# First expert's rows by one-hot products instead of a gather over DRAM, and the last row tile's affine part on TensorE and ScalarE

## The chip, the cores and the metric

One core of one Trainium2 chip runs the whole program. The metric is the time of one execution in device microseconds (us). The engines are named as in the profile: PE (TensorE, with PEld for its weight loads), DVE (VectorE), ACT (ScalarE), POOL (GpSimd) and SP (SyncE, which issues most transfers).

## The reference

One layer of an encoder on 512 tokens of 1024 channels. A token mixer (three linear-attention branches, merged by gates) ends in an output projection; its sum with the scaled input is normalised. A router then sends each token to two of 16 experts, each with two input matrices 1024 x 256 and one output matrix 256 x 1024; the weighted sum is added to the scaled tokens and normalised again. The part that matters here:

```
    mix = hybrid_mixer(h, ...)                     # ends in y @ w_out
    h = layer_norm(ALPHA * h + mix, ln1_g, ln1_b)  # the rows that are routed
    ffn = grouped_moe(h, ...)
    h = layer_norm(ALPHA * h + ffn, ln2_g, ln2_b)

def grouped_moe(x, ...):
    scores = sigmoid(t @ w_router)
    sel = (scores + router_bias).reshape(-1, 4, 4)          # 4 groups of 4 experts
    group_score = top_k(sel, 2)[0].sum(-1)                  # the best group,
    ...                                                     # the 2 best experts in it
    combine = one-hot of the 2 experts, times their scores over the sum
    h = silu(t @ w_gate[e]) * (t @ w_up[e])
    y = sum over e of (h * combine[e]) @ w_down[e]
```

## The kernel before

The 512 tokens are four row tiles of 128. The output projection is done in two column halves of 512. In the second half, `for n in range(NT)`, row tile n has four units (`wo_mm`, six matmuls each, float32 split in a high and a low part); between the units the steps of earlier row tiles are called. All instructions of this loop on TensorE are "pinned": each stays in its engine's queue behind the instruction that was written before it. Instructions that are not pinned are ordered by the framework's scheduler, by when their inputs are ready in its model.

`ln1(n)` holds the steps of one row tile: `half` adds the projection's result out of PSUM and takes statistics; `logits` transposes the tile and multiplies by the router; `scores` finds mean and inverse root and the sigmoid scores; `rows` applies gain and bias and stores the tile to `h1d` in DRAM. For the last tile 256 columns of the affine part run on DVE and 768 on ACT and POOL (multiply by the gain at L1263, add the bias at L1279).

`choose(n0, n1)` finds the experts of two row tiles on DVE: the mask `Mb`, and start values of `pos`; its inner `weigh` works out the weights. `ranks` multiplies the masks by a triangular matrix on PE and adds the result to `pos`, the place of a token among those of its expert. `slots` turns places into token numbers: for each expert a one-hot matrix (place equals slot, L1425) and small products of three columns (L1427, and L1436 for the weights). `gather` then fetches an expert's rows from `h1d` by an indirect transfer that POOL issues (L1449), and `ex_in` transposes them on PE (L1475).

`ex_up` multiplies by the input matrices in four units, each after a `split` of its raw weights into a high part (ACT, L316) and a low part (DVE, L317) in a ring of three pages. `ex_down` does the output matrix and scatters the result to `y2d` (L1507). The loop runs `ex_up(e)`, then `ex_down` of the expert before, then fetches the next expert. Raw weights come through a ring of 31 pages, so that about five experts are in stock when the loop begins. Between the last projection matmul and the first expert 66 matmuls on constants (L1536), which have no result that is used, are put on PE.

A float32 product appears in the trace as two matmuls each; a transpose as one.

Of the kernel before, what the change touches and what calls it, by code (L numbers as in the profile page):

```python
# [19 lines left out]
P = 128  # L20
# [18 lines left out]
def kernel(  # L39
# [1172 lines left out]
    raws = Ring(4)  # L1212
    for t in (whs, wls):
        t.i += 1
    def ln1(n):
# [12 lines left out]
        def half(c, psw):  # L1228
            cs = slice(c * T, (c + 1) * T)
            W.tensor_add(t[:, cs], t[:, cs], psw)  # L1230
            W.bn_stats(st[:, c], t[:, cs])

# [56 lines left out]
        return half, logits, scores, rows  # L1289
# [59 lines left out]
    def ranks():  # L1349

        ps = pst(pm)
        for n in range(NT):
# [4 lines left out]
        V.tensor_add(pos, pos, ps[:, :NT * E].rearrange("p (n e) -> p n e", e=E))  # L1357
# [18 lines left out]
    for n in range(NT):  # L1376
# [17 lines left out]
    half, logits, scores, rows = lns[3]  # L1394
    scores()
    rows()
    weigh = choose(2, 4, Pinned(V))
    ranks()
    drop(*x4)
    drop(*ah, *yT[0], *yT[1], g1r, b1r)  # L1400
# [7 lines left out]
    noh = [0]  # L1408
    raws = Ring(len(freed[F32]))
# [6 lines left out]
    def slots(es, pv, cv, gi, si, wi, mid=None, V=V):  # L1416

        m = len(es)
        ps, psw = pst(pm), pst(pm)
        oh = []  # L1420
        for j, e in enumerate(es):
# [4 lines left out]
            for n in range(NT):  # L1426
                TE.matmul(ps[:, 3 * j:3 * j + 3], o[:, n], cv(n, e)[:, 0:3], start=n == 0, stop=n == NT - 1)  # L1427
# [260 lines left out]
```

## Time and profile before

| | |
|---|---|
| median of 3 runs | 892.54 us (892.23 to 893.98) |
| the profiled execution, its own time | 893.27 us |
| its span | 891.6 us |
| mean granted clock of TensorE | 0.976 |
| PE busy | 831.9 us, 93% |
| DVE busy | 603.5 us, 68% |
| ACT busy | 442.3 us, 50% |
| POOL busy | 173.5 us, 19% |
| transfers | 126.05 MB, mean 141 GB/s |

The span reaches from the first to the last instruction that the profile records; the execution's own time is 1.7 us longer. Busy shares are means over stages with different limits. Mixer and branches take the first 620 us; the output projection ends at 670.55 us of the span, the experts run from about 691 to 860 us, and the last sum and normalisation take the rest.

### The profile page before, as it was taken

Reading aid. Unit: us, or ns where it says so; the run is one execution under the profiler, and the core shown is the slowest. Engines: PE = TensorE matmul, PEld = TensorE weight load, DVE = VectorE, ACT = ScalarE, POOL = GpSimd, SP = SyncE. Lnnn points to the kernel's source line nnn. Section 1 sums busy time; section 2 is a strip of 40 time slices with the busy share of each in tenths; the row PEclk is TensorE's granted clock in tenths of the full one; section 3 lists DMA queues with packets and bytes.
Section 4 is the critical chain, followed back from the end, with each engine's and each line's share of the span. In section 5 each row is a group of like instructions: output and inputs, shape, how many; then the busy total and the mean of one; then the engine's idle time right before and its main releaser. Section 6 shows DMA issues by size and latency. Waiting matters only on the chain.

```text
span 891.6 us, 15174 instructions
## 1 busy us (share of the span) xinstructions
PE 831.9 (93%) x5861; PEld 691.5 (78%) x5861; DVE 603.5 (68%) x1099; ACT 442.3 (50%) x823; POOL 173.5 (19%) x196
## 2 busy tenths in 40 slices
PE   8989999999989999999999999999998899999940
PEld 5867778978887999988888888888774777877730
DVE  7775566777675546686934346454469899989948
ACT  6533466654466443465323223233221688888833
POOL 2550001440361330201000000000023232222132
PEclk9989999999999999999999999999999999999985
DMA  6512322022013221244634334436635899997043
GB/s 196 136 54 74 86 69 60 25 75 70 25 72 119 72 71 49 72 129 133 187 111 127 95 98 142 119 119 214 234 119 172 269 364 353 362 365 289 27 168 134
DMA packets 100139, 126.05 MB, mean 141 GB/s; under 512 B 13072, under 2 KB 86880, under 8 KB 100064
## 3 DMA queue, kind: packets, MB, share of 16 engines
q1 hardware_dynamic: 89344, 109.17, 38.2%
q0 software_dynamic: 4608, 8.40, 2.6%
q10 hardware_dynamic: 6112, 7.48, 2.6%
q8 instruction: 47, 0.77, 0.4%
q14 instruction: 28, 0.23, 0.1%
HBM read 118.73 MB, written 14.68 MB: 150 GB/s over the span
## 4 chain that ended last, share of the span: by engine, by line
PE 70%; DVE 10%; issue 7%; DMA 5%; ACT 4%; POOL 3%; SPq 0%; DVEq 0%; ACTq 0%; POOLq 0%
PE ps L332 19%; PE ps L333 18%; PE ps L334 18%; PE ps L144 4%; DVE rr L317 2%; PE ps L906 1%; DMA ff<-in_w_gate_dram 1%; DVE ff L144 1%; PE ps L934 1%; PE ps L651 1%; PE ps L936 1%; PE ps L893 1%; ACT rr L316 1%; DMA ff<-in_w_down_dram 1%; POOL ff L713 1%
## 5 line engine op out<-in xcount | busy, mean ns | idle before, releaser
L317 DVE TENSOR_TENSOR rr<-ff,rr 128x1024 fp32r<-128x1024 f32 x148 | 183.4, 1246 | 117.3 <-ACT rr L316 114.5
L316 ACT CAST rr<-ff 128x1024 fp32r<-128x1024 f32 x150 | 157.0, 1054 | 178.6 <-PE ps L333 122.5
L332 PE MATMUL ps<-rh,rr 128*128 128x512 f32 x384 | 153.7, 400 | 0.0
L333 PE MATMUL ps<-rh,rr 128*128 128x512 f32 x384 | 150.5, 392 | 0.0
L334 PE MATMUL ps<-rh,rr 128*128 128x512 f32 x384 | 150.4, 392 | 0.0
L332 PE MATMUL ps<-rr,rh 128*128 128x256 f32 (+1 forms) x320 | 93.8, 293 | 0.6 <-DVE rh L144 0.6
L334 PE MATMUL ps<-rr,rh 128*128 128x256 f32 (+1 forms) x320 | 92.3, 289 | 1.5 <-issue 1.5
L333 PE MATMUL ps<-rr,rh 128*128 128x256 f32 (+1 forms) x320 | 91.9, 287 | 0.0
L332 PEld LDWEIGHTS ps<-rh,rr 128*128 128x128 f32 x384 | 72.4, 189 | 15.5 <-issue 0.8
L334 PEld LDWEIGHTS ps<-rh,rr 128*128 128x128 f32 x384 | 72.4, 189 | 15.5
L333 PEld LDWEIGHTS ps<-rh,rr 128*128 128x128 f32 x384 | 72.6, 189 | 14.1
L332 PEld LDWEIGHTS ps<-rr,rh 128*128 128x128 f32 x320 | 61.6, 192 | 3.2 <-issue 1.9
L334 PEld LDWEIGHTS ps<-rr,rh 128*128 128x128 f32 x320 | 61.3, 192 | 1.4 <-issue 0.8
L333 PEld LDWEIGHTS ps<-rr,rh 128*128 128x128 f32 x320 | 61.6, 193 | 0.3
L333 PE MATMUL ps<-rr,ro 128*128 128x512 f32 x128 | 52.2, 408 | 1.1 <-POOL rr L317 0.6
L332 PE MATMUL ps<-rr,ro 128*128 128x512 f32 x128 | 51.7, 404 | 0.3 <-issue 0.2
L334 PE MATMUL ps<-rr,ro 128*128 128x512 f32 x128 | 51.2, 400 | 0.7 <-DVE ro L1478 0.7
L1285 POOL TENSOR_TENSOR ff<-ff,ff 128x1024 f32<-128x1024 f32 x1 | 2.4, 2379 | 225.4 <-PE ps L144 225.4
L334 PE MATMUL ps<-ro,rr 128*128 128x512 f32 x96 | 37.4, 389 | 0.0
L332 PE MATMUL ps<-ro,rr 128*128 128x512 f32 x96 | 37.3, 389 | 0.0
L333 PE MATMUL ps<-ro,rr 128*128 128x512 f32 x96 | 37.3, 389 | 0.0
L1507 POOL DMA_INDIRECT y2d<-fl,sidx x16 | 20.8, 1300 | 71.5 <-ACT fl L1506 58.4
(550 smaller groups left out, 1681.8 us busy)
## 6 DMA issues: line engine op xcount, KB each, us to landing
ff<-in_w_in_dram SPq DMA_DIRECT2D x66, 512.0 KB
ff<-in_w_down_dram SPq DMA_DIRECT2D x25, 512.0 KB
ff<-in_w_gate_dram SPq DMA_DIRECT2D x41, 256.0 KB
ff<-in_w_up_dram SPq DMA_DIRECT2D x41, 256.0 KB
fh<-in_w_gate_dram SPq DMA_DIRECT2D x18, 256.0 KB
fh<-in_w_up_dram SPq DMA_DIRECT2D x18, 256.0 KB
ff<-in_w_out_dram SPq DMA_DIRECT2D x8, 512.0 KB
fh<-in_w_down_dram SPq DMA_DIRECT2D x6, 512.0 KB
```

The lines of the kernel that those rows point to most:

```text
L144: return lambda *a, **k: pin(f(*a, **k))
L316: S.copy(a, src)
L317: i = V.tensor_sub(b, src, a.bitcast(F32))
L332: TE.matmul(ps, w(0, k), h(0, k), start=start and k == k0, stop=False)
L333: TE.matmul(ps, w(0, k), h(1, k), start=False, stop=False)
L334: last = TE.matmul(ps, w(1, k), h(0, k), start=False, stop=stop and k == k1 - 1)
L651: tiny = lambda ps, lhs, rhs: [TE.matmul(half(ps)[u, i], lhs[u, i], rhs[u, i], start=True, stop=True) for i in range(NL) for u in B32]
L713: G.tensor_mul(ktok, ktok, bcol(ksc, NL))
L893: TE.matmul(p4[:, :, n], kd[:, g * NT + n], qd[:, g * NT + n], start=True, stop=True)
L906: TE.matmul(ps[:, c], kd[:, c], qd[:, c], start=True, stop=True)
L934: TE.matmul(po, atv(h)[:, n], vs[h][:, n], start=True, stop=n == 0)
L1507: s = nc.gpsimd.indirect_dma_start(out=y2d[:m], out_offset=bass.IndirectOffsetOnAxis(ap=sidx_col, axis=0), in_=yo, in_offset=None, bounds_ ...
```

## The change

The gather of the first expert's rows is replaced by products: with the tile's rows as the stationary side and a float32 one-hot matrix (token n in slot t, `oh0`) as the moving side, PE writes the transposed rows of expert 0 into PSUM (`rows0`), in two halves of four column blocks, over all four row tiles. `ranks` is called for two row tiles at a time, the first two inside the projection loop, and makes `oh0` as well. The gain multiply of the last row tile is put before its mean is known (`xg3`, POOL, by halves); mean and root are brought into a row by a transpose, and PE adds the identity times `xg3` and a two-row product of (minus mean, root) with (gain, bias); ACT scales by the inverse root on the way out of PSUM. `moments` is split off `scores`, and for the tile before the last it and `rows` are called two units earlier. The weights of the choice (`weigh`) and the slots of the experts 0, 2 and 3 are put behind expert 0's up products. The first three weight splits of expert 0 are called early. The 66 matmuls on constants are gone.

```diff
+    xg3, gb2, ohf = (new((P, D)) for _ in range(3))
+    for i, a in enumerate((ln1_g, ln1_b)):
+        nc.scalar.dma_start(gb2[i:i + 1], dram(a, 0, [[0, 1], [1, D]]))
+    oh0 = ohf[:, :T].rearrange("p (n t) -> p n t", t=P)
...
             W.bn_stats(st[:, c], t[:, cs])
+            if n == NT - 1:
+                G.tensor_mul(xg3[:, cs], t[:, cs], g1r[:, cs])
...
-            W.bn_aggr(mv[:, 0:2], flat(st))
-            W.tensor_scalar(nm, m, -1.0, None, op0=ALU.mult)
             if n == NT - 1:
-                S.activation(t[:, 256:], t[:, 256:], AF.Identity, bias=nm)
-                G.tensor_mul(t[:, 256:], t[:, 256:], g1r[:, 256:])
-                W.scalar_tensor_tensor(t[:, :256], t[:, :256], m, g1r[:, :256], op0=ALU.subtract, op1=ALU.mult)
-            r.append(rsqrt(mv[:, 1:2], 1, LN_EPS, 1.0, nm="rs1", V=W))
-            W.tensor_mul(mv[:, 3:4], nm, r[0])
+                moments()
...
-            if n == NT - 1:
-                W.scalar_tensor_tensor(t[:, :256], t[:, :256], r[0], b1r[:, :256], op0=ALU.mult, op1=ALU.add)
+        def moments():
+            W.bn_aggr(mv[:, 0:2], flat(st))
+            W.tensor_scalar(nm, m, -1.0, None, op0=ALU.mult)
+            r.append(rsqrt(mv[:, 1:2], 1, LN_EPS, 1.0, nm="rs1", V=W))
+            W.tensor_mul(mv[:, 3:4], nm, r[0])

         def rows():
             if n == NT - 1:
-                after(lambda: S.activation(t[:, 256:], t[:, 256:], AF.Copy, scale=r[0]))
-                G.tensor_add(t[:, 256:], t[:, 256:], b1r[:, 256:])
+                ms = nr0[:, 0, 0:2]
+                G.tensor_scalar(ms[:, 0:1], nm, 1.0, None, op0=ALU.mult)
+                G.tensor_scalar(ms[:, 1:2], mv[:, 1:2], LN_EPS, r[0], op0=ALU.add, op1=ALU.mult)
+                ps = pst(pm)
+                TE.transpose(ps[:2, :P], ms, ident)
+                mr = sm.tile([P, P], F32, name="mr", tag="sq", bufs=2)[:2]
+                after(lambda: S.copy(mr, ps[:2, :P]))
+                for c in range(2):
+                    cs = slice(c * T, (c + 1) * T)
+                    ps = pst(pp)
+                    TE.matmul(ps, ident, xg3[:, cs], start=True, stop=False)
+                    TE.matmul(ps, mr, gb2[:2, cs], start=False, stop=True)
+                    after(lambda: S.activation(t[:, cs], ps, AF.Copy, scale=r[0]))
...
-    def ranks():
+    def ranks(n0, n1, V):
         ps = pst(pm)
-        for n in range(NT):
+        for n in range(n0, n1):
...
-        V.tensor_add(pos, pos, ps[:, :NT * E].rearrange("p (n e) -> p n e", e=E))
+        V.tensor_add(pos[:, n0:n1], pos[:, n0:n1], ps[:, n0 * E:n1 * E].rearrange("p (n e) -> p n e", e=E))
+        V.tensor_tensor(oh0[:, n0:n1], slot[:, None, :].to_broadcast([P, n1 - n0, P]),
+                        pos[:, n0:n1, 0:1].to_broadcast([P, n1 - n0, P]), op=ALU.is_equal)
+
+    def rows0(q, n0, n1):
+        for n in range(n0, n1):
+            for c in range(4):
+                TE.matmul(xps[q][:, c * P:(c + 1) * P], ah[n][:, (4 * q + c) * P:(4 * q + c + 1) * P], oh0[:, n],
+                          start=n == 0 and c == 0, stop=n == NT - 1 and c == 3)
...
+            if u == (0 if n == NT - 1 else 2) and n:
+                lns[n - 1][4]()
             if u == 2 and n:
                 lns[n - 1][2]()
+            if u == (0 if n == NT - 1 else 2) and n:
                 lns[n - 1][3]()
-                if n == 2:
-                    choose(0, 2, V)()
+            if u == 2 and n == 2:
+                choose(0, 2, V)()
+                ranks(0, 2, V)
...
-    weigh = choose(2, 4, Pinned(V))
-    ranks()
+    xps += [pst(pp) for _ in range(2)]
+    W, TP = Pinned(V), Pinned(nc.tensor)
+    weigh = choose(2, 4, W)
+    for q in range(2):
+        rows0(q, 0, 2)
+    TE = TP
+    ranks(2, 4, W)
...
+    def parts(xT, q, ps, V=V):
+        qs = slice(4 * q, 4 * q + 4)
+        S.copy(flat(xT[0][:, qs]), ps)
+        V.tensor_sub(flat(xT[1][:, qs]), ps, flat(xT[0][:, qs]).bitcast(F32))
...
-    slots_of(0, 1, weigh, Pinned(V))
-    slots_of(1, 4, None, Pinned(V))
...
-    wts, xT = fetch(0)
-    ps = pst(pp)
-    with tc.issue_after(last.ins):
-        for i in range(66):
-            TE.matmul(ps.rearrange("p (a b) -> p a b", b=P), onb, onb[:, None, :].to_broadcast([P, NT, P]), start=True, stop=True)
+    first = [weights(0), weights(1)]
+    xT = [xTs((P, KD, P), F32R), xTs((P, KD, P), F32R)]
+    ready = []
+    def early(u):
+        with tc.issue_after(act[0].ins):
+            ready.append(split(first[0][u], pinned=True))
+    rows0(0, 2, 4)
+    rest = slots_of(1, 2, W, lambda: early(0))
+    rows0(1, 2, 4)
+    parts(xT, 0, xps[0], W)
+    early(1)
+    gather(xgs[1], gidx[:, 1:2])
+    parts(xT, 1, xps[1], W)
+    early(2)
+    wts = first[0]
     late = None
     for e in range(E):
...
-        ps = ex_up(xT, wts, pinned=e == 0, e=e)
+        TE = TP if e == 0 else nc.tensor
+        ps = ex_up(xT, wts, ready if e == 0 else (), e=e)
+        if e == 0:
+            weigh()
+            rest()
+            slots_of(0, 1, W)()
+            slots_of(2, 4, W)()
```

Smaller edits follow from these: `slots` returns its weight part as `rest`, `fetch` gathers from the second expert on only for e > 1, and some pages are released later.

## Rows read from the trace of the kernel before

**Rows 1.** Busy time of each engine by stage; then granted clock, DMA share, GB/s.
```profile
680.00:690.00 10.00, 7.54 (x67) 3.73 (x67) 8.90 (x35) 0.00 (x0) 1.75 (x2) 1.00 0.55 179
690.00:700.00 10.00, 7.76 (x62) 6.19 (x61) 6.11 (x11) 2.94 (x5) 3.48 (x3) 0.83 0.67 215
...
720.00:740.00 20.00, 19.93 (x104) 15.77 (x105) 19.05 (x26) 16.77 (x25) 5.09 (x4) 1.00 1.04 375
...
820.00:840.00 20.00, 19.64 (x96) 15.64 (x95) 18.35 (x22) 17.50 (x26) 1.96 (x2) 1.00 0.14 54
```

**Rows 2.** Timeline of ACT: output copies of the second and the fourteenth expert.
```profile
723.28 1.06 ACT L1506 COPY fl<-ps 128x512 f32<-128x512 f32 x2
...
843.37 1.08 ACT L1506 COPY fl<-ps 128x512 f32<-128x512 f32 x2
```

**Rows 3.** The chain that ended last, 640 to 730: start, us, what.
```profile
639.96 30.59 PE ps L144 x163
...
684.69 4.84 DMA fl<-h1d,gidx
```

**Rows 4.** Timeline behind the last projection matmul: start, us, engine, line, operation.
```profile
670.76 0.68 DVE L144 TENSOR_TENSOR ff<-ff,ps 128x512 f32<-128x512 f32 x1
...
672.54 0.48 DVE L144 SCALAR_TENSOR_TENSOR ff<-ff,mv,ff 128x256 f32<-128x256 f32 x1
...
673.86 0.16 DVE L144 SCALAR_TENSOR_TENSOR rs<-rs 128x1 f32<-128x1 f32 x1
...
674.11 1.81 POOL L1263 TENSOR_TENSOR ff<-ff,ff 128x768 f32<-128x768 f32 x1 [0.76 <-ACT ff L1262]
...
674.36 1.58 DVE L144 SCALAR_TENSOR_TENSOR rs<-rs 128x1 f32<-128x1 f32 x1
...
677.43 0.47 DVE L144 SCALAR_TENSOR_TENSOR ff<-ff,rs1o,ff 128x256 f32<-128x256 f32 x1
...
677.82 0.18 DVE L144 TENSOR_TENSOR scr<-sco,rb 128x32 f32<-128x32 f32 x1
...
678.55 0.28 DVE L144 TENSOR_TENSOR scr<-scr 128x128 f32<-128x128 f32 x1
678.66 1.83 POOL L1279 TENSOR_TENSOR ff<-ff,ff 128x768 f32<-128x768 f32 x1 [2.74 <-ACT ff L1278]
...
678.82 1.82 DVE L144 TENSOR_TENSOR scr<-scr,bef 128x128 f32<-128x128 f32 x1
...
681.83 0.17 PE L1356 MATMUL ps<-Mb,SUb 128*128 128x16 bf16 x1 [2.42 <-DVE Mb L144]
```

**Rows 5.** Timeline of PE and DVE at the first two experts.
```profile
691.45 0.58 PE L332 MATMUL ps<-rr,ro 128*128 128x512 f32 x1
...
695.07 1.09 PE L1475 MATMUL ps<-ident,fl 128*128 128x128 f32 x4 [2.24 <-DMA fl<-h1d,gidx]
...
695.81 0.78 PE L333 MATMUL ps<-rr,ro 128*128 128x512 f32 x1
...
699.45 1.23 DVE L317 TENSOR_TENSOR rr<-ff,rr 128x1024 fp32r<-128x1024 f32 x1 [3.67 <-ACT rr L316]
...
706.94 1.22 DVE L317 TENSOR_TENSOR rr<-fh,rr 128x1024 fp32r<-128x1024 f32 x1
```

**Rows 6.** Timeline of DVE: start of the weights, and three one-hots behind them.
```profile
683.90 0.19 DVE L144 TENSOR_TENSOR scr<-sco,Mb 128x32 f32<-128x32 f32 x1
...
686.14 1.88 DVE L144 TENSOR_TENSOR fl<-slot,pos 128x512 bf16<-128x512 f32 x3
```

**Rows 7.** Timeline of PE elsewhere: float32 products with 512 columns, and with 128 stationary columns.
```profile
275.08 1.98 PE L817 MATMUL ps<-ff 16*128 16x512 f32 x4
...
345.38 1.95 PE L893 MATMUL ps<-ff,ff 128*128 128x128 f32 x16
```

**Rows 8.** Timeline in row tile 2 of the projection: its last unit, and the choice.
```profile
660.45 1.66 PE L144 MATMUL ps<-ro,ry 128*128 128x512 f32 x6
...
661.18 0.19 DVE L1308 TENSOR_TENSOR scr<-sco,rb 128x32 f32<-128x32 f32 x1 [0.39 <-ACT sco L1272]
```

More of the change, by code (lines that the diff above doesn't have):

```diff
@@ L1287, in rows @@
             nc.sync.dma_start(h1d[n * P:(n + 1) * P], t)
-        return half, logits, scores, rows
+        return half, logits, scores, rows, moments
     def choose(n0, n1, V):
@@ L1393 @@
     TE = nc.tensor
-    half, logits, scores, rows = lns[3]
+    half, logits, scores, rows, _ = lns[3]
     scores()
     rows()
-    weigh = choose(2, 4, Pinned(V))
-    ranks()
+    xps += [pst(pp) for _ in range(2)]
[5 more added lines that the diff above has]
+    ranks(2, 4, W)
     drop(*x4)
-    drop(*ah, *yT[0], *yT[1], g1r, b1r)
+    drop(*yT[0], *yT[1], g1r, b1r)
     for t in (raws, whs, wls):
@@ L1408 @@
     noh = [0]
+    drop(xg3, gb2, ohf, *ah)
     raws = Ring(len(freed[F32]))
@@ L1427, in slots @@
                 TE.matmul(ps[:, 3 * j:3 * j + 3], o[:, n], cv(n, e)[:, 0:3], start=n == 0, stop=n == NT - 1)
+        if mid:
+            mid()
         t = sm.tile([P, m, 3], F32, name="slt")
@@ L1431, in slots, with rest @@
         V.scalar_tensor_tensor(si, t[:, :, 2], -OOB, gi, op0=ALU.add, op1=ALU.add)
-        if mid:
-            mid()
-        for j, e in enumerate(es):
-            for n in range(NT):
-                TE.matmul(psw[:, 3 * j:3 * j + 3], oh[j][:, n], cv(n, e)[:, 3:6], start=n == 0, stop=n == NT - 1)
-        V.tensor_reduce(wi, psw[:, :3 * m].rearrange("p (e c) -> p e c", c=3), axis=mybir.AxisListType.X, op=ALU.add)
+        def rest():
+            psw = pst(pm)
+            for j, e in enumerate(es):
+                for n in range(NT):
+                    TE.matmul(psw[:, 3 * j:3 * j + 3], oh[j][:, n], cv(n, e)[:, 3:6], start=n == 0, stop=n == NT - 1)
+            V.tensor_reduce(wi, psw[:, :3 * m].rearrange("p (e c) -> p e c", c=3), axis=mybir.AxisListType.X, op=ALU.add)
+        return rest
     xgs = []
@@ L1475, in ex_in, with ex_up @@
                 TE.transpose(ps[:, c * P:(c + 1) * P], xg[:, (4 * q + c) * P:(4 * q + c + 1) * P], ident)
-            qs = slice(4 * q, 4 * q + 4)
-            S.copy(flat(xT[0][:, qs]), ps)
-            V.tensor_sub(flat(xT[1][:, qs]), ps, flat(xT[0][:, qs]).bitcast(F32))
+            parts(xT, q, ps)
         return xT
-    def ex_up(xT, raw, pinned=False, e=0):
+    def ex_up(xT, raw, ready=(), e=0):
         ps = pst(pp)
         for u in range(4):
-            w = split(raw[u], pinned=pinned, V=G if e == E - 1 and u == 3 else V)
+            w = ready[u] if u < len(ready) else split(raw[u], V=G if e == E - 1 and u == 3 else V)
             mm3(ps, lambda b, k: xT[b][:, k], lambda b, k: w[b][:, k % 2], 2 * u, 2 * u + 2, u == 0, u == 3)
@@ L1513, in ex_down, with slots_of @@
         return sub
-    def slots_of(e0, e1, mid=None, V=V):
+    def slots_of(e0, e1, V=V, mid=None):
         es = slice(e0, e1)
-        slots(range(e0, e1), lambda e: pos[:, :, e:e + 1], lambda n, e: rc[:, n, e], gidx[:, es], sidx[:, es], wsl[:, es], mid, V)
-    slots_of(0, 1, weigh, Pinned(V))
-    slots_of(1, 4, None, Pinned(V))
+        return slots(range(e0, e1), lambda e: pos[:, :, e:e + 1], lambda n, e: rc[:, n, e], gidx[:, es], sidx[:, es], wsl[:, es], V, mid)
     gat = [None]
     def fetch(e):
-        wts = weights(e)
+        wts = weights(e) if e > 1 else first[e]
         if e % 4 == 1 and e < E - 4:
-            slots_of(e + 3, e + 7)
+            slots_of(e + 3, e + 7)()
         xg = xgs[e % 3]
-        gat[0] = gather(xg, gidx[:, e:e + 1])
+        if e > 1:
+            gather(xg, gidx[:, e:e + 1])
         return wts, ex_in(xg)
-    wts, xT = fetch(0)
-    ps = pst(pp)
-    with tc.issue_after(last.ins):
-        for i in range(66):
-            TE.matmul(ps.rearrange("p (a b) -> p a b", b=P), onb, onb[:, None, :].to_broadcast([P, NT, P]), start=True, stop=True)
+    first = [weights(0), weights(1)]
[13 more added lines that the diff above has]
+    wts = first[0]
     late = None
@@ L1546 @@
             wts, xT = fetch(e + 1)
+        TE = nc.tensor
     def at_end(src):
```

7 lines of the change are left out of this document (4 added, 3 removed).

## The prediction

> **What bounds the kernel now.** I read the stage table first. In the middle of the expert loop PE is busy 19.9 of 20 us and DVE 19.05 of 20 [rows 1]. The output copies of the second and the fourteenth expert start 120.1 us apart, so an expert takes 10.0 us [rows 2]. The weight transfers are over by 820 us while PE works on at 19.6 of 20 [rows 1]: they are a few experts ahead and set no end. So a gain at the start of the loop is kept to the end, and a change between the second output-projection half and the second expert is worth what it moves the loop.
>
> The chain of waits says what stands there: PE alone up to 670.55, and later 4.84 us from the issue of the first gather to its landing [rows 3]. The reader should see that PE has no gap before 670.55: any wait added there is paid in full.
>
> The timeline behind it shows three losses. A DVE instruction on one column takes 1.58 us, ending with a POOL multiply that began before it; a 128x128 multiply takes 1.82 us, ending with a POOL add [rows 4]. Then PE has the first matmul of expert 0 out at 691.45 but goes on only at 695.81, since its queue holds the transposes of expert 1, which wait 2.24 us for that expert's gather; the clock granted over 690 to 700 is 0.83 [rows 1, 5]. Last, DVE stands idle 3.67 us before the fourth split of expert 0, because PE is late [rows 5].
>
> **The change, part by part.** I keep the account on DVE, from the eviction of the last projection half (670.76) to the split of the last up unit of expert 1 (starts 706.94, takes 1.22, so ends 708.16): 37.4 us [rows 4, 5]. PE's next matmul waits for that split, so a shift of it shifts the loop.
>
> *Off POOL.* The multiply and the add over 768 columns go. The two DVE instructions that they held cost 1.58 - 0.16 = 1.42 (its unheld sisters are the length of 0.16) and 1.82 - 0.28 = 1.54: -3.0 us [rows 4]. The two 256-column instructions on DVE go too: 0.48 + 0.47 = -0.95 [rows 4].
> *Onto POOL.* A multiply of 512 columns follows the eviction; by the 1.81 us for 768 it takes 1.2. If it runs at once, DVE is in its statistics and nothing is held; if the three memsets that POOL has then go first, it meets the root's two-operand steps and holds one: 0 to +1.2. Taken: 0, as one memset at most should be in front. The Trainium skill ("SBUF — State Buffer", "Who interferes with whom") says that a DVE instruction with two SBUF inputs is shut out for the whole of a GpSimd instruction that reads SBUF, but not by one that only writes. The held rows agree with it, and by it the memsets hold nothing and the sum would be between the same two ends.
>
> *The gather goes.* With it goes DVE's idle time from 680 to 700: (10 - 8.90) + (10 - 6.11) = -5.0 us [rows 1].
> *New on DVE.* One one-hot of two row tiles in f32 (half of a 512-column one at 0.63, so 0.3) and a second addition to the positions (0.2), with pitch: +0.6 [rows 6].
> *New waits on DVE.* The sigmoid of the scores is no longer covered (0.4); the rank products (0.2); products of expert 0, ScalarE copy, subtraction twice (0.5 each); three reductions right behind their products (0.3 each); the fourth split of expert 0 behind PE and ScalarE (0.5 to 1). About 3.5; ends 2 and 5.
>
> *New on PE.* The same float32 product appears as two matmuls each: two programmed 512-column products took 1.98 us, eight with a 128-column stationary side 1.95 [rows 7]. So the four products for the last row tile cost about 4, and the 32 one-hot products 32 x 0.24 = 7.7, half of them before the choice is known. Between 670.6 and the one-hot PE gets about 9.5 us of work in a stretch of about 9; the 66 filler matmuls leave just this room. Price inside the 0.5 above; 0 to +1. The ScalarE copies of expert 0's splits move behind the row tile (3 x 1.05); ScalarE has nothing else there. Without that cover the first copy of the products would be late by up to 0.5.
>
> *The ranks of the first two row tiles* are the step that speaks against the change. They are called inside the loop over tile 2, where every TensorE instruction is pinned in program order, between unit 2 and unit 3 of the projection. Unit 3 now starts at 660.45, while the choice for those tiles starts only at 661.18 [rows 8]. It lasts as long as the later one, 677.82 to PE's first rank product at 681.83, less the held 1.54: 2.5 us [rows 4]. So the rank products start at 663.65, take 0.25, and unit 3 starts at 663.9: +3.4 us of PE standing still, with six projection matmuls, all of tile 3 and everything after it behind. Nothing before the change shows this wait; below, it cannot be under 0 and, if the clock falls in it, it is 3.4 + 1.7.
>
> *The slot work moves* behind expert 0's up products: weights with their reduction (683.90 to 686.14, 2.2 us), seven one-hots at 0.63 [rows 6], with the other reductions and index steps about 8.6 us on DVE. It is no new work, so it is in the account already; but the transposes of expert 1 are pinned behind all of it, and PE stands idle there for some 7 us. In the trace the clock fell to its lower level, 1.2 GHz, around the idle time of 2.24 us, behind a stretch of three-column products; a mean of 0.83 over 10 us is 1.7 us lost [rows 1, 5]. That loss happens in both kernels, in the new one nearer to the split that ends the account: +1.0 (0 to 1.7).
>
> *One-hots of experts 8 and 9* (two at 0.63), made ahead of the split at 706.94 now [rows 5, 6], will come later: -1.2 at the split, paid back in a loop where DVE has 5% free. Taken: -0.6.
>
> *DMAs.* The row store of the last tile and the gather of expert 1 stay; the store is about 2 us later, and the loads queued behind it on SP belong to the fourth and fifth expert, 30 us away. The two-row loads of gain and bias on ScalarE's queue are early and small. Without the stock of weights a late store would cost its 2 us. Nothing.
>
> **Sum.** -3.0 - 0.95 - 5.0 + 0.6 + 3.5 - 0.6 = -5.45 on DVE, +3.4 on PE, +1.0 for the clock: -1.05. The profiled execution took 893.27, so 892.2; the median of the three runs, 892.54, stands 0.73 below that execution: **891.5**.
>
> **The rivals.**
> *A, the head start survives.* PE's own start of expert 0 moves from 695.81 to about 687, some 9 us. If the choice is ahead of unit 3, or its wait is covered, the 3.4 falls away: 888.1; with the waits on DVE at their low end 886.6. For it: PE and DVE lose together more than 8 us between 680 and 700 [rows 1]. Against it: the pinned order leaves PE no other instruction.
> *B, the hand-over from expert 0 to expert 1 becomes the wait.* The 8.6 us of slot work stand in one fixed order before expert 1's transposes. I assume that its splits (four at about 1.2) fill DVE meanwhile or follow without gaps. If they come after it and wait again for PE and ScalarE, the new idle time is 7 rather than 3.5: 895.0, slower. It decides from 2.8 us of such idle time on. For it: DVE waited in the same manner for 3.67 us in the old order [rows 5]. Against it: these splits need only a weight page and a ring slot, both free by then.
> *C, the clock falls in the wait for the ranks too.* PE stands 3.1 us behind steady matmuls; if the granted clock falls there as it did before 695.81, another 1.7 us are lost: 893.2. The Trainium skill ("TensorE: Matmul & The Clock Gate", "Loop structure matters more than you think") warns that products which wait between bursts run cold; by it this rival, 893.2, would be the likeliest. The trace agrees in the one fall around 695 [rows 1, 5], and no row shows a wait in this place.
> *The gather was hidden anyway*: excluded, since PE waits for its landing in the chain [rows 3].
>
> **How the numbers follow.** A measurement of this kernel cannot tell less than about 0.2%, 1.8 us, from no change: same is 890.8 to 894.3. The forecast 0.30, its own range 889.5 to 893.0: 0.21 same, 0.09 faster. A 0.29, faster. B 0.28: 0.24 slower, 0.04 same. C 0.13: 0.12 same, 0.01 slower. So faster 0.38, same 0.37, slower 0.25. The range leaves out the ends of A and B: 886.5 to 896.0.
>
> **What would show it.** In the new profile: PE idle for about 3 us between units 2 and 3 of tile 2, ended by the choice's mask; no held DVE instruction in the root and the choice; the first product of expert 0 some 13 us behind the last projection matmul instead of 21; PE idle for 5 to 8 us before expert 1's transposes, with DVE busy; after that the old 10.0 us an expert. Wrong would make it: no wait at the ranks (then A), much idle DVE at the hand-over (then B), or an expert's time that changes by 0.2 us, which over 14 experts is 2.8 and outweighs all of this.

## The result, and the profile after

The changed kernel took 900.19 us (median of 4: 896.39, 899.09, 901.30, 901.31), the kernel before 893.1 beside it: a ratio of 1.0068, interval 1.0049 to 1.0087. It is slower by 0.7%, some 6 us, and lies outside the predicted range of 886.5 to 896.0. The profiled execution is the quickest of the four, 896.39, 3.1 us over the profiled execution before.

The rows that answer to [rows 1], by stage (PE, PEld, DVE, ACT and POOL busy with instructions, then the granted clock, DMA share, GB/s). The last row is the account of the prediction, from the eviction of the last projection half to the split of expert 1's last up unit:

```profile
660.00:665.00 5.00, 2.95 (x11) 2.38 (x11) 3.62 (x24) 0.00 (x0) 0.00 (x0) 0.69 0.01 2
680.00:690.00 10.00, 9.26 (x70) 7.52 (x69) 7.07 (x23) 5.37 (x7) 1.88 (x1) 1.00 0.70 246
690.00:700.00 10.00, 4.79 (x31) 3.64 (x29) 9.50 (x23) 5.87 (x6) 0.37 (x1) 0.97 0.93 324
700.00:710.00 10.00, 8.12 (x76) 7.09 (x77) 9.02 (x22) 3.47 (x5) 3.42 (x3) 0.68 0.99 361
...
673.74:709.97 36.23, 27.55 (x207) 22.15 (x206) 30.94 (x88) 15.74 (x21) 10.11 (x10) 0.91 0.87 308
```

The same account in the trace of before:

```profile
670.76:708.16 37.40, 32.12 (x221) 21.25 (x218) 31.82 (x85) 13.14 (x18) 12.36 (x10) 0.95 0.67 214
```

The timeline of PE, DVE and POOL of the changed kernel, answering to [rows 4, 5, 8] (start, duration, instruction; in brackets the wait and what ended it):

```profile
662.05 0.20 PE L144 MATMUL ps<-Mb,SUb 128*128 128x16 bf16 x1 [3.15 <-DVE Mb L1343]
...
662.15 2.91 PE L144 MATMUL ps<-ro,ry 128*128 128x512 f32 x6
...
673.77 0.95 POOL L1484 MEMSET fl<- 128x1024 f32 x1 [21.29 <-PE ps L144]
674.68 1.26 POOL L1238 TENSOR_TENSOR ff<-ff,ff 128x512 f32<-128x512 f32 x1
...
675.99 1.12 PE L1294 MATMUL ps<-ff,ident 128*128 128x512 f32 x2 [0.85 <-POOL ff L1238]
...
676.93 0.18 DVE L144 SCALAR_TENSOR_TENSOR rs<-rs 128x1 f32<-128x1 f32 x1
...
679.98 0.28 DVE L144 TENSOR_TENSOR scr<-scr,bef 128x128 f32<-128x128 f32 x1
...
680.51 1.98 PE L1295 MATMUL ps<-ff,mr 2*128 2x512 f32 x4
...
682.42 1.38 PE L1382 MATMUL ps<-ff,ff 128*128 128x128 f32 x10
...
684.00 0.19 DVE L144 TENSOR_TENSOR pos<-pos,ps 128x32 f32<-128x32 f32 x1 [2.06 <-PE ps L144]
...
684.70 2.05 PE L144 MATMUL ps<-ff,ff 128*128 128x128 f32 x16 [0.74 <-DVE ff L144]
...
688.48 5.73 PE L144 MATMUL ps<-rr,ro 128*128 128x512 f32 x24
...
694.05 0.20 PE L144 MATMUL ps<-rc,fl 128*128 128x3 bf16 x2
...
697.43 0.19 PE L144 MATMUL ps<-rc,fl 128*128 128x3 bf16 x2 [3.18 <-DVE rc L144]
...
700.68 0.27 PE L144 MATMUL ps<-rc,fl 128*128 128x3 bf16 x4 [1.85 <-DVE fl L144]
...
703.67 1.95 PE L144 MATMUL ps<-ident,fl 128*128 128x128 f32 x8
```

Four things are to be seen. PE stands 3.15 us at the ranks of the first two row tiles, and the projection unit behind them takes 2.91 us instead of 1.66 [rows 8]: the granted clock fell, 0.69 over 660 to 665. The step that POOL held is 0.28 long now, where it was 1.82 [rows 4]. In its place DVE waits 2.06 us for the rank products, which stand on PE behind the two-row products (1.98 us) and ten one-hot matmuls (1.38). And PE, done with expert 0's ups at 694.05, has only three-column products until 703.67, and waits between them for DVE, which is busy 9.50 of 10.

To place the loss, I cut the profiled executions at the same instructions. A is the start of row tile 2's unit 2 to that of unit 3 (units counted from 0), B from there to the end of the last projection product, C to the start of expert 0's output copy, D from there to the copy of the last expert, E to the end of the span. The kernels of the experiments, described below, stand in the same table.

| us | A | B | C | D | E | ratio to before, interval |
|---|---|---|---|---|---|---|
| before | 2.19 | 10.11 | 41.46 | 147.16 | 32.42 | |
| after | 5.51 | 11.55 | 40.41 | 148.50 | 32.09 | 1.0068 (1.0049 to 1.0087) |
| e1_ranks_late | 2.19 | 10.16 | 48.96 | 148.33 | 32.43 | 1.0077 (1.0052 to 1.0102) |
| e2_expert1_first | 5.51 | 14.43 | 46.61 | 150.59 | 32.56 | 1.0130 (1.0105 to 1.0155) |
| e4_both | 2.18 | 10.16 | 50.83 | 149.94 | 33.20 | 1.0133 (1.0111 to 1.0155) |
| e3_fill_wait | 5.48 | 10.04 | 41.59 | 148.25 | 33.83 | 1.0061 (1.0038 to 1.0084) |
| e5_before_ranks_early | 5.49 | 10.05 | 42.02 | 148.56 | 32.07 | 1.0065 (1.0049 to 1.0081) |
| i3_before_ranks_fill | 5.47 | 10.05 | 42.43 | 147.20 | 33.79 | 1.0033 (1.0018 to 1.0048) |
| f1_before_no_fill | 2.19 | 10.11 | 44.13 | 147.23 | 32.92 | 1.0019 (1.0007 to 1.0031) |
| f3_mul_first | 2.19 | 10.16 | 42.86 | 148.40 | 33.16 | 1.0020 (1.0004 to 1.0036) |
| g1_slots_late | 5.49 | 13.21 | 39.41 | 149.54 | 33.16 | 1.0084 (1.0063 to 1.0104) |
| h1_late_mul_fill | 2.18 | 10.16 | 41.43 | 148.43 | 33.32 | 1.0009 (0.9998 to 1.0019) |
| h2_late_mul_fill_slots | 2.18 | 10.16 | 39.58 | 149.48 | 33.33 | 0.9994 (0.9984 to 1.0004) |
| i1_ranks_first | 2.18 | 10.16 | 39.36 | 149.49 | 32.43 | 1.0000 (0.9987 to 1.0013) |
| h5_before_affine | 2.19 | 10.10 | 40.23 | 148.30 | 32.98 | 0.9986 (0.9976 to 0.9996) |
| i2_affine_ranks_first | 2.18 | 10.11 | 39.84 | 148.65 | 33.94 | 1.0000 (0.9987 to 1.0013) |
| j1_affine_mul_first | 2.19 | 10.10 | 38.22 | 148.62 | 32.52 | 0.9975 (0.9960 to 0.9990) |

From before to after: A +3.32, B +1.44, C -1.05, D +1.34, E -0.33, together +4.72; the stretch ahead of A, which the change does not touch, happened to be 1.62 shorter in this execution, hence +3.1. The table holds one execution a kernel; the ratios hold all of them, but for one execution of the kernel before that took 2869 us, beside i1, i2 and i3. C and D belong together, since the order in which the first copies come differs between kernels: from the last projection product to the last expert's copy it is 188.62 us before and 188.91 after. So behind the projection the changed kernel won nothing, and what its profiled execution lost lies in A and B.

### The profile page after: what moved, and what is told of

It reads as the page before. It is cut to its first block, busy times and chain, and to the rows that moved or that the text cites. A ratio compares the mean times of both kernels' runs of the same rounds, so it can differ in the third digit from the quotient of the medians.

```text
span 894.7 us, 15185 instructions
## 1 busy us (share of the span) xinstructions
PE 829.8 (93%) x5860; PEld 694.0 (78%) x5860; DVE 603.9 (68%) x1104; ACT 442.9 (50%) x824; POOL 169.4 (19%) x197
## 5 line engine op out<-in xcount | busy, mean ns | idle before, releaser
L332 PE MATMUL ps<-rr,ro 128*128 128x512 f32 x120 | 48.5, 404 | 0.8 <-ACT ro L1513 0.7
L333 PE MATMUL ps<-rr,ro 128*128 128x512 f32 x120 | 48.3, 402 | 0.8 <-POOL rr L317 0.6
L334 PE MATMUL ps<-rr,ro 128*128 128x512 f32 x120 | 47.7, 398 | 0.6 <-DVE ro L1514 0.6
L1238 POOL TENSOR_TENSOR ff<-ff,ff 128x512 f32<-128x512 f32 x2 | 2.6, 1278 | 213.4 <-DVE ff L144 213.4
L434 DVE SCALAR_TENSOR_TENSOR scr<-ps,vcol,scr 128x511 f32<-128x511 f32 (+2 forms) x36 | 26.7, 743 | 10.7 <-ACT scr L431 10.1
```

The lines of the kernel that those rows point to most:

```text
L332: TE.matmul(ps, w(0, k), h(0, k), start=start and k == k0, stop=False)
L333: TE.matmul(ps, w(0, k), h(1, k), start=False, stop=False)
L334: last = TE.matmul(ps, w(1, k), h(0, k), start=False, stop=stop and k == k1 - 1)
L434: V.scalar_tensor_tensor(y[:, sh:], ps[:, :T - sh], convw[:, j, j0:j0 + 1], y[:, sh:], op0=ALU.mult, op1=ALU.add)
L1238: G.tensor_mul(xg3[:, cs], t[:, cs], g1r[:, cs])
```

## The experiments

Each is timed against the kernel before. The expectations speak of theories and rivals. Theory 1: two waits, at the early ranks and ahead of expert 1, and the half clock behind them make the loss. Rival 2: the period of the experts' loop makes it. Rival 3: the new float32 products and the affine part on other engines make it. Theory 4 came later: the loss is time at half clock.

**e1_ranks_late: the ranks of the first two row tiles moved into the last row tile, behind its unit 1.**

```diff
             if u == 2 and n == 2:
                 choose(0, 2, V)()
+            if u == 1 and n == NT - 1:
                 ranks(0, 2, V)
```

> The changed kernel, but the rank products of the first two row tiles stand behind the last unit of tile 2's projection instead of between its second and third (at the second unit of tile 3). Theory 1 (two waits and their clock make the loss): TensorE no longer waits 3.15 us for Mb, unit 3 takes 1.7 instead of 2.91 us, the granted clock of 660 to 665 us is 1.0 instead of 0.69; the last projection product ends about 4.5 us earlier, and the time falls by 4 to 5 us against the changed kernel, to about the kernel before +1.5. Rival 2 (the period of the experts' loop makes the loss): nothing but this wait moves, and what is won here is lost again ahead of expert 1, so under 1 us of gain. Rival 3 (the new float32 products and the affine part on the other engines make the loss): under 1 us, since none of them is touched.

1.0077, 901.3 us: nothing won, where theory 1 had 4 to 5 us. The wait is gone (A 2.19, B 10.16), but C is 48.96, 8.55 longer than in the changed kernel. The timeline shows where it went:

```profile
669.54 2.73 POOL L1485 MEMSET fl<- 128x1024 f32 x3 [16.55 <-PE ps L144]
672.24 1.26 POOL L1238 TENSOR_TENSOR ff<-ff,ff 128x512 f32<-128x512 f32 x1
...
672.89 0.63 DVE L144 SCALAR_TENSOR_TENSOR rs<-rs 128x1 f32<-128x1 f32 x1
...
673.55 1.65 PE L1294 MATMUL ps<-ff,ident 128*128 128x512 f32 x2 [1.96 <-POOL ff L1238]
...
681.12 1.98 PE L1295 MATMUL ps<-ff,mr 2*128 2x512 f32 x4
...
685.08 0.19 DVE L144 TENSOR_TENSOR pos<-pos,ps 128x32 f32<-128x32 f32 x1 [4.83 <-PE ps L144]
...
685.78 3.78 PE L144 MATMUL ps<-ff,ff 128*128 128x128 f32 x16 [0.74 <-DVE ff L144]
...
692.04 5.72 PE L144 MATMUL ps<-rr,ro 128*128 128x512 f32 x24
```

All three memsets go ahead of the gain multiply, and PE waits 1.96 us for it. The mean clock of the 20 us from 670 on is low:

```profile
670.00:680.00 10.00, 7.44 (x31) 5.96 (x31) 7.52 (x36) 1.27 (x4) 4.00 (x6) 0.70 0.67 241
680.00:690.00 10.00, 9.26 (x52) 7.67 (x52) 2.84 (x8) 4.60 (x6) 0.00 (x0) 0.67 0.59 192
```

These means hide two falls. Read in steps of 2 us the clock is 0.50 from 674 to 680, behind the wait for the multiply, 1.00 from 682 to 684, and 0.50 again from 686 to 690, behind a wait of 0.74 us for DVE. In between, the two-row products take 1.98 us, as in the changed kernel; in the second fall sixteen one-hot matmuls take 3.78 us, where the changed kernel has 2.05. DVE's wait for the rank products grows from 2.06 to 4.83. In the changed kernel one memset went ahead and PE's wait was 0.85.

**e2_expert1_first: expert 1's ups ahead of the slot work.**

```diff
-        if e % 4 == 1 and e < E - 4:
+        if e % 4 == 1 and 1 < e < E - 4:
...
-        if e == 0:
+        if e == 1:
             weigh()
             rest()
             slots_of(0, 1, W)()
             slots_of(2, 4, W)()
+            slots_of(4, 8)()
```

> The changed kernel, but the weights and slots of the first experts are worked out behind expert 1's up products instead of behind expert 0's, and the one-hots of experts 4 to 7 with them. Theory 1: TensorE goes from expert 0's ups to expert 1's transposes without the 9.6 us (694.05 to 703.67) in which it had only small products between waits for DVE, and the granted clock of 700 to 710 us is not 0.68; expert 1's ups end 3 to 6 us earlier than at 711.56, and the time falls by as much, unless expert 0's downs, which need the weights, then wait. A second view of theory 1, that VectorE's work (9.5 of 10 us busy from 690 to 700) is the bound and only changes its order: 0 to 2 us of gain. Rival 2 (loop period): 0, and the yo copies of expert 13 stay as far behind those of expert 1 (122.9 us against 120.1 before).

1.0130, 906.89 us: by the ratios 5.5 us worse than the changed kernel. The wait moves and is not removed; first the transposes wait for the gather, then the slot products for DVE:

```profile
700.28 1.09 PE L144 MATMUL ps<-ident,fl 128*128 128x128 f32 x8 [3.25 <-DMA fl<-h1d,gidx]
...
712.33 0.19 PE L1475 MATMUL ps<-rc,fl 128*128 128x3 bf16 x2 [3.15 <-DVE rc L144]
```

The gather was issued at 690.96, so 9.3 us passed to its landing; the first gather of the kernel before took 4.84 [rows 3]. C grows by 6.2. So expert 1's ups come too early for their gather: the order of the change is the better of the two. **e4_both**, this edit with that of e1, gave 1.0133 (1.0111 to 1.0155), the highest ratio of all, against the 7 to 10 us of gain that theory 1 had.

> Both edits together: the late rank products and expert 1 ahead of the weights and slots. Theory 1: 7 to 10 us under the changed kernel, that is some 1 to 4 us under the kernel before. If VectorE is the bound of the hand-over: the gains do not add, 4 to 5 us, level with the kernel before or just above it. Rivals 2 and 3: under 1 us.

**e3_fill_wait: twelve constant products before the early ranks**, so that PE is not idle while it waits.

```diff
+                pf = pst(pm)
+                for i in range(12):
+                    TE.matmul(pf.rearrange("p (a b) -> p a b", b=P), onb, onb[:, None, :].to_broadcast([P, NT, P]), start=True, stop=True)
                 ranks(0, 2, V)
```

> The changed kernel with 12 products of a constant (512 columns each, about 2.6 us) on TensorE in the place where it waits 3.15 us for Mb. They compute nothing that is used. If the half clock behind the wait (0.69 in 660 to 665 us, unit 3 at 2.91 instead of 1.66 us) comes of the idle time: unit 3 back at 1.7 us, the clock at 1.0, and 1 to 1.5 us of gain. If the wait alone is the loss and the clock falls for another reason: no gain, or 0.3 us of loss. Theory 1 says 1 to 1.5 us of gain here against 4 to 5 for taking the wait away; rivals 2 and 3 say nothing changes.

1.0061, 899.11: by the ratio 0.6 us less than the changed kernel, with overlapping intervals, so no gain that this can tell. The unit behind takes 1.62 us (B 10.04), A is still 5.48:

```profile
662.41 0.17 PE L144 MATMUL ps<-Mb,SUb 128*128 128x16 bf16 x1 [0.45 <-DVE Mb L1343]
662.49 1.62 PE L144 MATMUL ps<-ro,ry 128*128 128x512 f32 x6
```

**e5_before_ranks_early: the kernel before, with only the ranks split and the first two called early.**

```diff
-    def ranks():
+    def ranks(n0, n1, V):
...
                 choose(0, 2, V)()
+                ranks(0, 2, V)
...
-    ranks()
+    ranks(2, 4, V)
```

> The kernel before with one part of the change alone: the rank products of the first two row tiles stand between the second and third unit of tile 2, the others stay where they were. Nothing else is changed. If a pinned wait there costs its length: TensorE waits about 3.2 us for Mb, the last projection product ends 3 us later, and the time rises by 3 us. If the clock falls with it, as in the changed kernel (0.69 in 660 to 665 us): 4.5 to 5 us. If what comes behind it has slack (the moved wait of the late rank products in the changed kernel gave nothing), under 1.5 us.

1.0065, 900.09 us: this one edit costs 5.8 us, as much as the whole change. **i3_before_ranks_fill** puts the twelve constant products of e3 before this call:

> The kernel before with the early ranks alone (900.1 us, 6 over the kernel before), and 12 products of a constant in TensorE's 3.15 us of waiting. They compute nothing that is used. If half of the 6 us is half-clock time behind the wait: 2 to 3 us of gain, to about 897.5. If the wait as such delays what follows by 6 us: under 1 us.

1.0033, 897.46: by the ratios 2.9 us come back and 2.9 stay, about what A grew by (5.47 against 2.19); the two intervals lie just apart. So in e5 the standing queue costs some 3 us and what follows from an idle PE about as much. That this is half clock is argued: the mean clock of e5's six executions is 0.971 and that of i3's twelve 0.975, but a mean clock alone proves little, as f1 below shows. The profiled execution of e5 is its quickest and shows no low clock behind the wait (first row); the profile of g1 below, whose projection is that of the changed kernel, does (the other rows):

```profile
665.00:670.00 5.00, 5.00 (x30) 4.01 (x29) 4.13 (x15) 1.66 (x3) 0.00 (x0) 1.00 0.05 17
...
660.00:665.00 5.00, 1.85 (x14) 1.36 (x13) 3.56 (x22) 0.70 (x2) 0.00 (x0) 1.00 0.26 105
665.00:670.00 5.00, 5.00 (x19) 4.29 (x19) 3.48 (x18) 0.00 (x0) 0.00 (x0) 0.57 0.01 2
670.00:675.00 5.00, 5.00 (x23) 3.73 (x22) 2.47 (x8) 0.59 (x1) 0.00 (x0) 0.74 0.00 0
```

After the same wait of 3.15 us B is 10.05 in e5, 11.55 in the changed kernel, 13.21 in g1 and 14.43 in e2: the price of the clock is 0 to 4.3 us over 10.1, by execution. That agrees with the four times of the changed kernel, of which the slower have the lower mean clock (0.970 against 0.975, and 0.005 x 897 = 4.5 of the 4.9 us between them).

**f1_before_no_fill: the kernel before without its 66 constant products.**

```diff
-        for i in range(66):
-            TE.matmul(ps.rearrange("p (a b) -> p a b", b=P), onb, onb[:, None, :].to_broadcast([P, NT, P]), start=True, stop=True)
```

> The kernel before with another part of the change alone: the 66 products of a constant between the projection and the first expert are taken out. They compute nothing that is used, so what they take from the time is only what they do to TensorE's clock. New theory 4 (the loss is half-clock time: TensorE waits where the fillers kept it busy, and what follows runs at half clock): the granted clock of 670 to 700 us falls to about 0.6, the time rises by 1.5 to 4 us, and the product of span and mean clock stays at 869 to 870 us as in the kernel before. Rival (fillers are worth nothing, since TensorE only waits there): under 0.5 us.

1.0019, 896.36: they are worth 1.7 us (0.0019 x 893). Without them the clock is 0.50 over 680 to 690, where PE has only 1.92 us of work to slow down, and over 690 to 700, where it has 8.56 and the clock before was 0.83 [rows 1]:

```profile
680.00:690.00 10.00, 1.92 (x37) 1.43 (x36) 8.87 (x31) 0.00 (x0) 2.84 (x2) 0.50 0.65 207
690.00:700.00 10.00, 8.56 (x46) 6.99 (x47) 7.89 (x12) 2.48 (x4) 3.54 (x3) 0.50 0.58 182
```

The expected product of span and mean clock, 869 to 870 us, did not hold: it is 864 (895.8 x 0.965), since part of the low clock met an idle PE.

**f3_mul_first: e1, with POOL's memsets held behind the gain multiply.**

```diff
-                G.tensor_mul(xg3[:, cs], t[:, cs], g1r[:, cs])
+                gm[0] = G.tensor_mul(xg3[:, cs], t[:, cs], g1r[:, cs])
...
-        G.memset(t, 0.0)
+        with tc.issue_after(gm[0].ins):
+            G.memset(t, 0.0)
```

> The kernel with the late rank products, and besides it the three memsets of POOL stand behind the gain multiply of the last row tile instead of in front of it. With the late ranks alone TensorE waited 1.96 us for that multiply, the clock of 670 to 690 us was 0.68, and all products of the affine part and of the first expert's rows took twice as long. Theory 4: without this wait the clock of 670 to 690 us is 1.0, expert 0's ups start at about 685 instead of 692.0 us, and the time falls by 4 to 6 us against the late ranks alone, to 895 to 897. Rival (the clock is low there because float32 products with 128 columns are too little work, wait or not): no gain over 0.5 us and a clock of 0.7 again.

1.0020, 896.92: by the ratios 5.1 us better than e1 and 4.3 better than the changed kernel. So the late ranks do remove most of the loss, once the memsets are out of the way; the memsets' order without the late ranks was not run in the changed kernel. The wait for the multiply is 0.69 us, and the clock still falls later:

```profile
673.49 1.12 PE L1294 MATMUL ps<-ff,ident 128*128 128x512 f32 x2 [0.69 <-POOL ff L1238]
...
682.19 3.68 PE L144 MATMUL ps<-ff,ff 128*128 128x128 f32 x16 [0.74 <-DVE ff L144]
```

```profile
680.00:690.00 10.00, 9.26 (x63) 8.59 (x63) 6.14 (x11) 5.55 (x8) 2.25 (x1) 0.83 0.65 209
```

**g1_slots_late: the changed kernel with the slots of experts 4 to 7 found one expert later.**

```diff
-        if e % 4 == 1 and e < E - 4:
-            slots_of(e + 3, e + 7)()
+        if e % 4 == 2 and e < E - 3:
+            slots_of(e + 2, e + 6)()
```

> The changed kernel, but the one-hots and index products of experts 4 to 7 are called one expert later (and those of 8 to 11 and 12 to 15 likewise), so that they don't stand in TensorE's pinned order ahead of expert 1's transposes. If the hand-over is bound by the order in which VectorE's slot work stands ahead of expert 1: transposes of expert 1 at about 701.3 instead of 703.7 us and 2 to 3 us of gain. If the half clock is what is lost there: under 1 us, with 0.68 again around expert 1's transposes. If VectorE as a whole is the bound of the first experts: what is won here comes back in the loop, 0 to 1 us.

1.0084: no gain. C is 1.0 shorter and D 1.0 longer; what is put off is done in the loop.

**h1_late_mul_fill: f3, with 26 constant products in the waits** (3 behind the second ranks, 13, 3 and 7 in the slot work), and **h2_late_mul_fill_slots: the same with the edit of g1.**

> The kernel with the late rank products and the multiply ahead of the memsets, and besides it products of a constant in TensorE's waits: 3 behind the last rank products, 13, 3 and 7 behind expert 0's ups, where TensorE waits 0.74, 3.2, 0.85 and 1.8 us for VectorE. They compute nothing that is used and fit in the waits. Theory 4 (half-clock time): the clock of 680 to 710 us, now 0.83, 0.79 and 0.69, is 1.0; expert 0's second half of products 2.0 instead of 3.7 us, expert 1's transposes 1.05 instead of 1.95 us; 2 to 3.5 us of gain against the same kernel without them, to the time of the kernel before or just under it. Rival (VectorE's order bounds the hand-over, TensorE's speed there is hidden): under 1 us, with the clock at 1.0.

> As the one above (late ranks, multiply first, constant products in the waits), with the one-hots of experts 4 to 7 called one expert later as well. If that step alone lost its gain only to half-clock time: another 1 to 2 us under the one above. If VectorE as a whole bounds the first experts: within 0.5 us of it.

1.0009 and 0.9994: level with the kernel before. The clock of h1 is 1.00 from 670 to 700, with the sixteen one-hot matmuls at 2.05 us. That speaks against f3's rival, by which these products have a low clock, wait or no wait:

```profile
680.00:690.00 10.00, 9.93 (x64) 8.37 (x63) 9.22 (x16) 6.42 (x9) 2.25 (x1) 1.00 0.86 274
690.00:700.00 10.00, 7.86 (x90) 4.42 (x89) 9.38 (x29) 2.66 (x4) 1.00 (x1) 1.00 1.05 366
...
680.34 2.05 PE L144 MATMUL ps<-ff,ff 128*128 128x128 f32 x16
```

Expert 0's ups begin at 684.12 there, 15.3 us behind the projection against 20.9 before [rows 5], and yet C is 41.43 against 41.46. The head start of PE is real and brings nothing. The step from h1 to h2 is 1.3 us, with intervals that overlap.

**h5_before_affine: the kernel before with the affine part alone** (multiply on POOL, products, ACT's scale; 50 constant products for 66).

```diff
+            if n == NT - 1:
+                G.tensor_mul(xg3[:, cs], t[:, cs], g1r[:, cs])
...
-                S.activation(t[:, 256:], t[:, 256:], AF.Identity, bias=nm)
-                G.tensor_mul(t[:, 256:], t[:, 256:], g1r[:, 256:])
-                W.scalar_tensor_tensor(t[:, :256], t[:, :256], m, g1r[:, :256], op0=ALU.subtract, op1=ALU.mult)
...
+                    TE.matmul(ps, ident, xg3[:, cs], start=True, stop=False)
+                    TE.matmul(ps, mr, gb2[:2, cs], start=False, stop=True)
+                    after(lambda: S.activation(t[:, cs], ps, AF.Copy, scale=r[0]))
```

> The kernel before with the third part of the change alone: gain multiply on POOL before the mean is known, identity and two-row products on TensorE, scale on ScalarE for the last row tile; gather, ranks and slots stay, and 50 of the 66 products of a constant. My prediction's terms: VectorE is rid of 1.42 + 1.54 us of holding and of 0.95 us of work, so the choice for the last tiles ends 3 to 4 us earlier, and the time falls by as much as the gather does not wait for the row store instead: -1 to -3.5 us. Rival 3 (the affine part on the other engines costs as much as it saves: four products of 512 columns behind TensorE's other work, two ScalarE passes, then the store): the store of the last tile is no earlier than at 680.5 us, the gather lands when it did, and the time stays within 1 us.

0.9986, 892.81: this part is a gain, a small one. DVE waits for PE here too:

```profile
672.17 1.12 PE L1287 MATMUL ps<-ff,ident 128*128 128x512 f32 x2 [1.59 <-POOL ff L1236]
...
680.71 0.22 DVE L1367 TENSOR_TENSOR pos<-pos,ps 128x64 f32<-128x64 f32 x1 [3.05 <-PE ps L1366]
```

**i1_ranks_first and i2_affine_ranks_first** put the two-row products behind the rank products, in h2 and in h5, to take this wait away (i2 also has 40 constant products, 10 of them ahead, where h5 has 50):

```diff
-                    TE.matmul(ps, mr, gb2[:2, cs], start=False, stop=True)
-                    after(lambda: S.activation(t[:, cs], ps, AF.Copy, scale=r[0]))
+                def affine():
+                    for c in range(2):
+                        cs = slice(c * T, (c + 1) * T)
+                        TE.matmul(pa[c], mr, gb2[:2, cs], start=False, stop=True)
+                        after(lambda: S.activation(t[:, cs], pa[c], AF.Copy, scale=r[0]))
```

> The changed kernel with late ranks, multiply first, constant products behind expert 0 and slots one expert later, and besides it the two-row products of the last row tile (2 us on TensorE) behind the rank products of the last two tiles instead of ahead of them. Now VectorE has the mask at 677.2 us and waits 1.9 us for TensorE, which still works on those. If this queue eats what VectorE wins: the wait falls under 0.5 us, expert 0's ups start 1 to 2 us earlier, and the time falls by 1 to 2 us, to about 891.5 to 892.5. If the products are only late in another place (rows of the last tile later by 2 us, and the first expert's products wait for them): no gain.

> The kernel before with the affine part alone, where VectorE waited 3.05 us for the rank products behind TensorE's two-row products (choice done at 677.1, places at 680.7 us): the two-row products now stand behind the rank products, and 40 of the 66 products of a constant are left, 10 of them ahead. If the queue eats it: the wait falls to about 0.5 us, the index of the first gather is there 2 to 2.5 us earlier, and the time falls by 1 to 2.5 us against the affine part alone. If the store of the last tile's rows, which comes after those products, sets the gather: no gain, 0 to 1 us.

Both 1.0000: nothing won. In i2 the wait shrinks to 0.77, but DVE's next three waits grow from 0.35, 0.28 and 1.93 in h5 to 1.15, 1.19 and 2.78: 2.56 us more behind it, where 2.28 were won. First i2, then the last of these waits in h5:

```profile
679.14 0.22 DVE L1372 TENSOR_TENSOR pos<-pos,ps 128x64 f32<-128x64 f32 x1 [0.77 <-PE ps L1371]
...
692.36 1.29 DVE L1497 TENSOR_TENSOR ro<-ps,ro 128x512 fp32r<-128x512 f32 x2 [2.78 <-ACT ro L1496]
...
691.24 1.29 DVE L1489 TENSOR_TENSOR ro<-ps,ro 128x512 fp32r<-128x512 f32 x2 [1.93 <-ACT ro L1488]
```

**j1_affine_mul_first: h5, with the memsets behind the multiply** (the edit of f3).

> The kernel before with the affine part alone and POOL's three memsets behind the gain multiply, which TensorE waited 1.59 us for. If this wait and the half clock behind it limit the part: the multiply starts 1 us earlier, the clock of 670 to 680 us is 1.0 instead of 0.83, and the time falls by 1 to 2 us against the affine part alone, to 891 to 892. If the rank products behind TensorE's queue or the store of the last tile's rows limit it: under 0.5 us.

0.9975 (0.9960 to 0.9990), 892.1: faster than both kernels, 0.25% below before and 0.9% below the changed kernel (0.9975 / 1.0068). From h5 it can't be told for sure: the two intervals overlap. PE waits 0.69 for the multiply instead of 1.59, DVE 1.10 for the ranks instead of 3.05, and C is 38.22:

```profile
671.23 1.13 PE L1288 MATMUL ps<-ff,ident 128*128 128x512 f32 x2 [0.69 <-POOL ff L1237]
...
678.43 0.22 DVE L1368 TENSOR_TENSOR pos<-pos,ps 128x64 f32<-128x64 f32 x1 [1.10 <-PE ps L1367]
```

## Why the prediction was wrong

**The step that failed is the sum on DVE**: -5.45 with +1.0 for the clock, so -4.45 expected; the account went from 37.40 to 36.23, so -1.17. DVE's busy time in it fell by 0.88, not by 3.95. Of the 3.1 between, 2.0 are one-hots: I took those of experts 8 and 9 to come later (-0.6), and the groups show 12 of 512 columns in the account instead of 10, at 0.69 each (+1.4). Of the other 1.1 the groups show a fourth set of index steps (four of 0.16, in slot work that I had as no new work) and expert 0's 256-column product (0.42), less a score row of 0.23 that now lies ahead of the account; the rest I could not tie to single rows. Here are the eight one-hots of the changed kernel and the six of the kernel before; both kernels have four more at L144:

```profile
L1461 DVE TENSOR_TENSOR fl<-slot,pos 128x512 bf16<-128x512 f32 x8 | 5.4, 686 | 0.0
```

```profile
L1425 DVE TENSOR_TENSOR fl<-slot,pos 128x512 bf16<-128x512 f32 x6 | 4.1, 680 | 0.0
```

DVE's idle time fell by 0.29, not by 1.5 (5.0 less 3.5). I had the new waits at 3.5 together, none above 1; the one for the rank products is 2.06 alone.

**Held DVE instructions: right.** None is left (0.28 for 1.82, and the root's step 0.18 for 1.58). What they freed came to the choice, and then went into the wait for the ranks. With one memset in front, as I assumed, nothing is held on DVE. With three, in e1, the multiply holds one root step (0.63 for 0.16), within my bound of 0 to +1.2; what I had at nothing is PE's wait for the multiply, 0.85 with one memset in front and 1.96 with three.

**PE's new float32 work: mis-sized at nothing.** I put 9.5 us of it in a stretch of 9 and priced the overlap inside a wait of 0.5 on DVE. It is the 2.06 us: DVE has the mask at 681.40, and PE is still at the two-row products (1.98 us) and ten one-hot matmuls (1.38) that stand ahead of the rank products.

**The ranks: right as a wait, too small in all.** 3.4 us were predicted, A shows 3.32, but by e5 the early ranks cost 5.8 us. Rival C, that the clock falls there too, came true in the changed kernel's profile (+1.44 in B), and its price is 0 to 4.3 us rather than 1.7. I gave it 0.13, too little, though its 893.2 lies 7 us under the measured time as well. The Trainium skill ("TensorE: Matmul & The Clock Gate", "Loop structure matters more than you think") has matmuls run cold where a long wait for a transfer stands between them. The changed kernel's 0.69 and the 2.9 us between e5 and i3 agree with it; e5's profile, with the same wait and a clock of 1.00, does not, and in e3 the constant products gave nothing to be measured.

**The hand-over: right in its mechanism, not in size.** PE has no product but those of three columns for 9.6 us (694.05 to 703.67) where I had 7, with DVE busy 9.50 of 10, as forecast and against rival B, whose idle DVE did not come. The ups of expert 0 begin 14.8 us behind the projection (688.48 - 673.70; 13 predicted, 20.9 before). Rival A's head start is there, but it doesn't survive: in h1 it is nearly as large, without the early ranks, and C is that of before. That DVE, which has hardly less to do in this stretch (34.65 us busy in C against 35.88), holds it is how I read it; no run shows it by itself.

**The loop: nearly as assumed.** D grew by 1.34 us over 15 experts, 0.09 an expert where 0.2 would have upset the forecast. By the copies that the prediction went by, the second (724.13) and the fourteenth (846.06), the loop takes 121.9 us against 120.1, or 0.15 more an expert: nearer to the sign of being wrong, and not over it. D grew as much in e5, h5 and j1, whose loop is that of before, and not in f1 and i3, whose loop is so too: it is not the change's own, and what sets it is open.

Put together for the profiled executions, -1.05 was expected and +4.72 came: 3.4 of the difference from the sum on DVE (C -1.05 against -4.45, here to expert 0's copy), 1.4 from the clock behind the ranks, 1.0 from D and E. The ratio gives 6.1 us, 1.4 more; the executions with a lower mean clock have no profile, so that it is the clock behind the ranks again is argued from g1 and e2, not shown. Taken with D, C gave nothing at all: 188.91 us against 188.62.

**What stays open.** What decides whether the clock falls in a given wait; why the same products gave 2.9 us in i3 and nothing in e3; and where the one-hot rows, the core of the change, would pay. With all mends (h2) the kernel with them is level with before; j1, without them, is faster than before, by an interval that overlaps that of h2. The one-hot rows were not run alone.

## What to carry to other kernels

A call placed in a loop whose matmuls are pinned in order is a wait for whatever it reads: compute when its input is there, and when the matmul behind it would start, and count the half clock that can follow beside the wait itself. When an engine is relieved in a chain that passes through three of them, price the next engine's queue first: what DVE gained from POOL here, it waited for PE. And time the parts of a change one by one: the part that looked least (the affine part with a sane memset order) was the only gain.

## What the runs showed of the hardware

The granted clock does not follow the length of a wait alone: 3.15 us in front of the same unit cost nothing in e5's profile (clock 1.00), and 14.43 us against 10.11 for the units behind it in e2's, where the row shows the lower of the two levels, 1.2 GHz, with PE busy throughout:

```profile
665.00:670.00 5.00, 5.00 (x20) 4.31 (x19) 2.03 (x8) 0.00 (x0) 0.00 (x0) 0.50 0.00 0
```

In e1 it fell twice within 20 us, behind waits of 1.96 and 0.74 us, and was 1.00 in between; in the changed kernel the same wait of 0.74 us was followed by no fall (sixteen one-hot matmuls in 2.05 us).

A DVE step that met a POOL multiply or add ended with it or within 0.15 us of it: 1.58 and 1.82 us in the kernel before [rows 4], 0.63 in e1. Where POOL was at no such instruction, the same steps took 0.18 and 0.28 us in the changed kernel.
